# The low parts of 36 mixer weights, made during the feed-forward layer's way down and stored, instead of beside the recurrence

## The chip, the cores and the metric

The kernel runs on one core of one Trainium2 chip. The metric is the device time of one execution in microseconds (us). Six units are spoken of: PE (TensorE matmuls), PEld (TensorE's loading of weights, beside the matmuls), DVE (VectorE), ACT (ScalarE), POOL (GpSimd) and SP (SyncE, which issues almost every DMA here and does nothing else). Each takes its instructions in a fixed order and stops at the first one whose inputs aren't there.

## The reference

One layer of a diffusion transformer over 1152 columns (1024 latent tokens and 128 of context), width 1024, in fp32, for latents and context with the same weights:

```
x += 1/2 * gate1 * SwiGLU1(adaLN(RMSNorm(x)))        # first feed-forward half step
x += gate2 * W_out( sig(g_a)*Up_a(MLA(h)) + sig(g_r)*Up_r(HGRN2_bidir(h)) ),  h = adaLN(RMSNorm(x))
x += 1/2 * gate3 * SwiGLU2(adaLN(RMSNorm(x)))        # second feed-forward half step
...
def swiglu(h, w1, w3, w2):
    return (jax.nn.silu(h @ w1) * (h @ w3)) @ w2
...
qc, kvc, kr, hq, hf_f, hf_b, hi, hgate, ga, gr = jnp.split(h @ w_in, split_idx, axis=-1)
```

The change touches two places: the product with `w2` in the first half step (2816 hidden rows to 1024), called the way down, and the first 36 tiles of `w_in` (1024 x 128 each), which feed the HGRN2 recurrence and the gates `ga` and `gr`.

## The kernel before

Full fp32 accuracy is made out of three fp32r matmuls. A matrix A is split into a high part Ah (A rounded to fp32r, a cast on ACT) and a low part Al = A - Ah (a subtraction, mostly on POOL); the product is wh·xh + wh·xl + wl·xh (`mm3`, L455, L456, L457). Line 238 and line 239 in `hl` make the high and the low part of a weight tile; lines 1624 and 1625 those of a hidden tile (`hh`, `hl`).

The way down (`ffn_fast`, then `down_group` and `down_last`): 22 hidden tiles of 128 x 1152 are loaded from DRAM (`hr`, 576 KB), split (`hh`, `hl`), and multiplied with 22 rows of `w2` (`raw`, 512 KB, split into `wh`, `wl` for even and `wxh`, `wxl` for odd rows). They go in pairs: 9 groups of two tiles, called group 0 to 8 here, then `down_last` with the last four. A group has 24 ticks (8 row blocks m, 3 chunks of 384 columns); a tick is 6 matmuls into one bank (`dn`) and then one to three additions to `x` on DVE (L484), scaled from the bank. At every third tick a background generator (`self.bg`, `ada_sum`) takes one step: a load of 256 KB (`wada`) and a reduction on DVE (`junk`, L308). The bank has three buffers, hidden tiles two groups' worth, `wh` and `wl` three, `raw` two.

The recurrence (`hgrn`) runs the HGRN2 scans of eight heads level by level. DVE carries most of it (`KE`, `QP`, `T`, `A`), POOL takes part of it (`QP`, `Y`), and PE's small matmuls (`lv`, L860) wait for these. Beside it run 36 dense products, one per tile of `w_in` (`proj_f`, `proj_q`, `proj_v`, `proj_gate`, `proj_sg`); each loads its weight, casts `wh` on ACT and subtracts `wl` on POOL. For the very first tile the two halves of `wl` are made on DVE (`home="pieces"`).

The order of each engine's instructions is set once, when the program is built, by a scheduler that follows the order of the code, the priorities and the pools' buffers; at run time nothing passes anything on the same engine. All loads and stores spoken of here go through SP's queue.

Of the kernel before, what the change touches and what calls it, by code (L numbers as in the profile page):

```python
# [9 lines left out]
F32 = mybir.dt.float32  # L10
F32R = mybir.dt.float32r
# [8 lines left out]
P = 128  # L20
D = 1024
KT = D // P
# [8 lines left out]
ORDER = (2, 0, 1)  # L31
# [31 lines left out]
def rows(w, m):  # L63

    return w[m // 4][:, ts(m % 4, P)] if isinstance(w, list) else w[:, 0, ts(m, P)]
# [22 lines left out]
class Trunk:  # L88
# [1 line left out]
        self.tc, self.nc, self.a, self.o = tc, tc.nc, a, o  # L90

    def run(self):
        self.part, self.mode, self.chunks, self.bg = {}, "ffn1", ORDER, iter(())
        nc, tc, a = self.nc, self.tc, self.a
        with ExitStack() as st:
            self.cp = st.enter_context(tc.tile_pool(name="cp", bufs=1))
            self.wp = st.enter_context(tc.tile_pool(name="wp", bufs=1))
            self.tp = st.enter_context(tc.tile_pool(name="tp", bufs=25))
            self.dp = st.enter_context(tc.tile_pool(name="dp", bufs=1, space=DRAM))
            self.consts()  # L100
            self.xs = self.dp.tile([KT, P, T], F32, name="xs")
            self.modt = self.cp.tile([P, 9, KT, 2], F32, name="modt")
            self.gs = self.cp.tile([P, 3, KT, 2], F32, name="gs")
            with ExitStack() as s1:
                self.ffn_pools(s1)
                self.start()
                self.ffn_fast(0, 2, 1)
            self.mode = "mix"
            with tc.tile_pool(name="mp", bufs=1) as mp:
                self.mixer_consts(mp)  # L110
                self.mixer()
            with ExitStack() as s1:
                self.mode = "ffn2"
                self.ffn_pools(s1)
                self.merge()
                self.ffn_fast(1, 8, 3)
# [101 lines left out]
    def hl(self, raw, shape, eng=None, pin=lambda i: i, home=None):  # L218
        if home == "half":
            wh, wl = [[self.half(n, F32R)[:, : D // 2] for _ in range(2)] for n in ("wxh", "wxl")]  # L220
            for v in range(2):
                src = raw[:, 0, ts(v, D // 2)]
                self.nc.scalar.copy(wh[v], src)
                self.nc.gpsimd.tensor_sub(wl[v], src, wh[v])
            return wh, wl
        if home == "pieces":
            wh, wl = [self.wp.tile(shape, F32R, tag=t, bufs=3, name=t) for t in ("wh", "wl")]
            for v in range(2):
                k = slice(4 * v, 4 * v + 4)
                self.nc.scalar.copy(wh[:, k], raw[:, k])  # L230
                self.nc.vector.tensor_sub(wl[:, k], raw[:, k], wh[:, k])
            return wh, wl
        if home:
            wh, wl = [home(n)[:, :D].rearrange("p (o d) -> p o d", o=1) for n in ("wxh", "wxl")]
        else:
            wh = self.wp.tile(shape, F32R, tag="wh", bufs=3, name="wh")
            wl = self.wp.tile(shape, F32R, tag="wl", bufs=3, name="wl")
        pin(self.nc.scalar.copy(wh, raw))  # L238
        pin((eng or self.nc.gpsimd).tensor_sub(wl, raw, wh))  # L239
        return wh, wl  # L240

    def load_w(self, src, kt, m, pin=lambda i: i, home=None):
        raw = self.wp.tile([P, kt, m], F32, tag="raw", bufs=2, name="raw")
        self.nc.sync.dma_start(raw, src)
        return self.hl(raw, [P, kt, m], None, pin, home)
# [247 lines left out]
    def down_group(self, w2, fs, hs, gm, ws=None):  # L493
        ws = ws or [self.load_w(w2[f], 1, D) for f in fs]
        for m in range(KT):
            for c in self.chunks:
                self.down([(rows(wh, m), rows(wl, m)) for wh, wl in ws], hs, gm, c, m)
                self.ticks += 1
                if self.ticks % 3 == 0:
                    next(self.bg, None)  # L500

    def down_last(self, w2, fs, hs, gm, nxt):
        n = len(fs)
        self.new_rs()
        o = (0, 3, 1, 2)
        spare = "half" if nxt < 3 else partial(self.wide, dt=F32R)
        ws = [self.load_w(w2[fs[i]], 1, D, home=spare if i == 3 else None) for i in o]
        hs = [hs[i] for i in o]
        if nxt == 3:
            self.down_final(ws, hs, gm)  # L510
            return
        nc = self.nc
        if nxt == 2:
            self.alloc_b(1)
        else:
            self.alloc_h()
        tail = iter(())
        for c in self.chunks:
            cs = slice(*span(c))
            for m in range(KT):  # L520
                self.down([(rows(wh, m), rows(wl, m)) for wh, wl in ws], hs, gm, c, m)
                self.stat(c, m)
                nc.sync.dma_start(self.xs[m][:, cs], self.x[m][:, cs])
                if m:
                    next(tail, None)
            for _ in tail:
                pass
            tail = self.norm(c, nxt)
        self.tail = tail
# [103 lines left out]
    def proj_f(self, i, h, out):  # L633
        nc = self.nc
        fs = out["f"] = self.tt(F32, "fs")
        nc.vector.memset(fs[64:P, 0:1], 1.0)
        w = self.load_w(self.a["w_in"][i], KT, P, home="pieces" if i == 0 else None)
        for c in ORDER:
            s = self.sigm((yield from self.proj_g(w, c)))
            lo, hi = c * CW, (c + 1) * CW  # L640
            for r, o in ((slice(0, 64), 0), (slice(64, P), 1)):
                nc.scalar.activation(
                    fs[r, lo + o : hi + o], s[r], AF.Identity, scale=self.lb1[r, h : h + 1], bias=self.lb[r, h : h + 1]
                )
            yield

    def proj_q(self, i, out):
        q = out["q"] = self.tt(F32, "q")
        w = self.load_w(self.a["w_in"][i], KT, P)
        for c in ORDER:  # L650
            ps = yield from self.proj_g(w, c)
            self.nc.vector.tensor_mul(q[:, c * CW : (c + 1) * CW], ps, self.sigm(ps))  # L652
            yield

    def proj_v(self, i, out):
        nc = self.nc
        V = out["V"] = self.tt(F32, "V")
        w = self.load_w(self.a["w_in"][i], KT, P)
        for c in ORDER:
            ps = yield from self.proj_g(w, c)  # L660
            t = self.fp.tile([P, CW], F32, tag="t", bufs=3, name="t")
            nc.scalar.copy(t, ps)
            pt = self.pp.tile([P, CW], F32, tag="sm", bufs=3, name="vt")
            for j in range(3):
                nc.tensor.transpose(pt[:, ts(j, P)], t[:, ts(j, P)], self.ident)
            nc.scalar.copy(V[:, c * CW : (c + 1) * CW], pt)
            yield

    def proj_gate(self, i, p, oT):
        nc = self.nc  # L670
        w = self.load_w(self.a["w_in"][i], KT, P)
        sq = self.tt(F32, "osq")[:, :T]
        nc.scalar.activation(sq, oT[:, :T], AF.Square)
        for c in ORDER:
            ps = yield from self.proj_g(w, c)
            if c == ORDER[0]:
                self.lnexp()
                for b in ORDER:
                    self.rec_norm(b, oT, sq)
            s = self.sigm(ps)  # L680
            nc.vector.tensor_mul(s, ps, s)
            cs = slice(c * CW, (c + 1) * CW)
            nc.gpsimd.tensor_mul(s, oT[:, cs], s)
            nc.sync.dma_start(self.orec[p][:, cs], s)
            yield

    def proj_sg(self, j):
        w = self.load_w(self.a["w_in"][20 + j], KT, P)
        for c in ORDER:
            s = self.sigm((yield from self.proj_g(w, c)))  # L690
            self.nc.sync.dma_start(self.sg[j // KT, j % KT][:, c * CW : (c + 1) * CW], s)
            yield
# [876 lines left out]
    def ffn_fast(self, l, gm, nxt):  # L1569

        nc = self.nc
# [6 lines left out]
        for f in range(plain):  # L1578
# [7 lines left out]
            n = 0  # L1586
# [44 lines left out]
        for f in range(plain, NF):  # L1631
# [3 lines left out]
            for n in range(7):  # L1635
                if len(made) < 6:
                    w = next(ops, None)
                    if w:
                        made.append(w)
                w = made.pop(0)  # L1640
# [20 lines left out]
            self.put(*t)  # L1661
        self.x += [load_x(k) for k in range(2, KT)]
        if l == 0:
            self.bg = self.ada_sum((6, 7), lambda: self.bank("up", "cb", D // 2), partial(self.tt, F32), self.slim)
        for f in range(2, NF):
            pend.append(split_h(*load_h(f)))
            if f % 2 and f < NF - 1:
                fs, hs = zip(*pend[:2])
                self.down_group(w2, fs, hs, gm, ws or [load_w2(v) for v in fs])
                pend, ws = pend[2:], None  # L1670
        for _ in self.bg:
            pass
        fs, hs = zip(*pend)
        self.down_last(w2, fs, hs, gm, nxt)
# [122 lines left out]
```

## Time and the profile before

| what | value |
|---|---|
| median of 3 runs | 2986.64 us (2986.32 to 2988.35) |
| the profiled execution | 2991.17 us, span 2989.4 us |
| mean granted clock of TensorE | 0.986 of full |
| PE busy | 2882.2 us (96%) |
| DVE busy | 2034.1 us (68%) |
| ACT busy | 1242.1 us (42%) |
| POOL busy | 1084.1 us (36%) |
| groups 0 to 8 of the first way down | 558.0 to 785.9 us, 25.1 us a group |
| `down_last` | 785.9 to 839.4 us |
| the recurrence with its 36 products | 839.5 to about 1460 us |

Times inside the program are counted from the span's start. Where the table of a stretch gives an engine less busy time than the stretch is long, the rest is idle time; only PE's counts towards the end directly. In rows of the timeline the bracket at the end is how long the engine was idle before, and what ended that.

### The profile page before, as it was taken

Reading aid. Unit: us, or ns where it says so; the run is one execution under the profiler, and the core shown is the slowest. Engines: PE = TensorE matmul, PEld = TensorE weight load, DVE = VectorE, ACT = ScalarE, POOL = GpSimd, SP = SyncE. Lnnn points to the kernel's source line nnn. Section 1 sums busy time; section 2 is a strip of 40 time slices with the busy share of each in tenths; the row PEclk is TensorE's granted clock in tenths of the full one; section 3 lists DMA queues with packets and bytes.
Section 4 is the critical chain, followed back from the end, with each engine's and each line's share of the span. In section 5 each row is a group of like instructions: output and inputs, shape, how many; then the busy total and the mean of one; then the engine's idle time right before and its main releaser. Section 6 shows DMA issues by size and latency. Waiting matters only on the chain. (4 is left out here: it accounts for less than half of the span.)

```text
span 2989.4 us, 49363 instructions
## 1 busy us (share of the span) xinstructions
PE 2882.2 (96%) x18498; PEld 2737.8 (92%) x18498; DVE 2034.1 (68%) x4206; ACT 1242.1 (42%) x2375; POOL 1084.1 (36%) x979
## 2 busy tenths in 40 slices
PE   7999999999989999999998999989999999999998
PEld 5999999999989989898997887779999999999997
DVE  7787777677668787877456677766674665546665
ACT  5432332321274555555244777731362233232113
POOL 4132322454153333323234444532342322236434
PEclk8999999999999999999998999999999999999999
DMA  6643333743111111111210000242352322235211
GB/s 231 203 147 122 121 129 115 250 158 117 61 58 60 35 53 38 51 38 44 66 51 12 14 17 20 65 155 90 117 180 97 106 88 74 74 117 203 90 45 64
DMA packets 151471, 282.37 MB, mean 94 GB/s; under 512 B 19201, under 2 KB 83649, under 8 KB 151233
## 3 DMA queue, kind: packets, MB, share of 16 engines
q1 hardware_dynamic: 151088, 278.90, 28.2%
q8 instruction: 146, 2.39, 0.3%
q14 instruction: 93, 0.75, 0.1%
q10 hardware_dynamic: 144, 0.33, 0.0%
HBM read 215.64 MB, written 63.52 MB: 93 GB/s over the span
## 5 line engine op out<-in xcount | busy, mean ns | idle before, releaser
L1547 PE MATMUL b<-xo,wo 128*128 128x288 f32 x3552 | 484.7, 296 | 0.0
L1547 PEld LDWEIGHTS b<-xo,wo 128*128 128x128 f32 x3552 | 476.5, 188 | 0.0
L484 DVE SCALAR_TENSOR_TENSOR x<-dn,modt,x 128x256 f32<-128x256 f32 (+4 forms) x728 | 353.2, 505 | 167.9 <-PE dn L457 167.0
L239 POOL TENSOR_TENSOR wl<-raw,wh 128x1024 fp32r<-128x1024 f32 (+1 forms) x106 | 240.3, 2268 | 371.5 <-ACT wh L238 357.7
L455 PE MATMUL mm<-xh,wh 128*128 128x384 f32 (+1 forms) x1008 | 361.6, 359 | 5.7 <-DVE q L652 3.7
L1547 PE MATMUL b<-bh,wo 128*128 128x288 f32 x1776 | 365.2, 295 | 0.7 <-ACT et L1557 0.7
L457 PE MATMUL mm<-xh,wl 128*128 128x384 f32 (+1 forms) x1008 | 342.6, 340 | 1.7 <-POOL wl L239 1.5
L456 PE MATMUL mm<-xl,wh 128*128 128x384 f32 (+1 forms) x1008 | 343.0, 340 | 0.0
L1547 PEld LDWEIGHTS b<-bh,wo 128*128 128x128 f32 x1776 | 288.7, 188 | 1.0 <-ACT et L1557 0.9
L1547 PE MATMUL b<-bl,wo 128*128 128x288 f32 x888 | 261.6, 295 | 0.0
L1522 ACT CAST wo<-raw 128x512 fp32r<-128x512 f32 x185 | 114.8, 621 | 231.2 <-PE b L1547 114.5
L238 ACT CAST wh<-raw 128x1024 fp32r<-128x1024 f32 (+1 forms) x108 | 104.3, 967 | 250.6 <-PE dn L456 166.1
L455 PEld LDWEIGHTS mm<-xh,wh 128*128 128x128 f32 (+1 forms) x1008 | 190.9, 189 | 15.6 <-DVE q L652 4.5
L455 PE MATMUL dn<-hh,wh 128*128 128x384 f32 (+2 forms) x576 | 196.0, 340 | 2.6 <-DVE x L484 1.3
L1523 DVE TENSOR_TENSOR wo<-raw,wo 128x512 fp32r<-128x512 f32 x185 | 127.1, 688 | 102.2 <-ACT wo L1522 99.3
L457 PE MATMUL dn<-hh,wl 128*128 128x384 f32 (+2 forms) x576 | 194.2, 337 | 1.0 <-POOL wl L239 1.0
L456 PE MATMUL dn<-hl,wh 128*128 128x384 f32 (+2 forms) x576 | 194.1, 337 | 0.0
L457 PEld LDWEIGHTS mm<-xh,wl 128*128 128x128 f32 (+1 forms) x1008 | 190.4, 189 | 3.5 <-POOL wl L239 2.0
L456 PEld LDWEIGHTS mm<-xl,wh 128*128 128x128 f32 (+1 forms) x1008 | 190.9, 189 | 1.6 <-issue 0.4
L1625 POOL TENSOR_TENSOR hl<-hr,hh 128x1152 fp32r<-128x1152 f32 x44 | 118.0, 2692 | 196.9 <-ACT hh L1624 103.7
L1279 POOL TENSOR_TENSOR ehl<-e,ehl 128x512 fp32r<-128x512 f32 x93 | 123.3, 1330 | 142.9 <-ACT ehl L1277 77.3
L1518 POOL TENSOR_TENSOR ws<-raw 128x256 f32<-128x256 f32 x74 | 68.5, 945 | 292.9 <-DMA raw<-in_w 265.8
(385 smaller groups left out, 7284.9 us busy)
## 6 DMA issues: line engine op xcount, KB each, us to landing
raw<-in_w SPq DMA_DIRECT2D x148, 256.0 KB, 2.9
raw<-in_w SPq DMA_DIRECT2D x58, 512.0 KB, 3.6
wada<-in_w_aT SPq DMA_DIRECT2D x112, 256.0 KB, 2.9
hr<-hs SPq DMA_DIRECT2D x44, 576.0 KB, 5.1
hs<-et SPq DMA_DIRECT2D x148, 144.0 KB, 1.7
raw<-in_w_in SPq DMA_DIRECT2D x41, 512.0 KB, 3.5
hb<-hd SPq DMA_DIRECT2D x44, 288.0 KB, 3.4
x<-in_xT SPq DMA_DIRECT2D x16, 576.0 KB, 8.7
```

Of the source, the lines that this page charges most:

```text
L238: pin(self.nc.scalar.copy(wh, raw))
L239: pin((eng or self.nc.gpsimd).tensor_sub(wl, raw, wh))
L455: nc.tensor.matmul(ps, wh, xh, start=start and i == 0, stop=False)
L456: nc.tensor.matmul(ps, wh, xl, start=False, stop=False)
L457: nc.tensor.matmul(ps, wl, xh, start=False, stop=stop and i == n - 1)
L484: nc.vector.scalar_tensor_tensor(self.x[m][:, a:b], ps[:, a - lo : b - lo], self.modt[:, gm, m, s : s + 1], self.x[m][:, a:b], ALU.mult, A ...
L1279: eng.tensor_sub(el, e, eh)
L1518: nc.gpsimd.tensor_tensor(o[:, c], x[:, c], y[:, c], op)
L1522: nc.scalar.copy(wh, src[i])
L1523: nc.vector.tensor_sub(wl, src[i], wh)
L1547: nc.tensor.matmul(ps, w[:, k], x[:, k, :QW], start=first, stop=last, skip_group_check=home != i)
L1625: nc.gpsimd.tensor_sub(hl, raw, hh)
```

## The change

A second generator, `low_parts`, takes a step at every tick whose number leaves 1 when divided by 3. For each of the 36 weights it loads the raw tile once more (`wraw`, 512 KB), casts each half to a scratch (`whi`, 128 x 512, ACT), subtracts that in place (128 x 512, POOL), and stores the result (512 KB) to a new DRAM tile `wlo`. A weight's store is issued within the next weight's steps. In the recurrence `load_in` loads the raw tile as before and the low part from `wlo`, and casts `wh`; POOL's subtraction is gone, and so are DVE's two halves for the first tile.

```diff
             self.xs = self.dp.tile([KT, P, T], F32, name="xs")
+            self.wlo = self.dp.tile([36, P, D], F32, name="wlo")
...
-        if home == "pieces":
-            wh, wl = [self.wp.tile(shape, F32R, tag=t, bufs=3, name=t) for t in ("wh", "wl")]
-            for v in range(2):
-                k = slice(4 * v, 4 * v + 4)
-                self.nc.scalar.copy(wh[:, k], raw[:, k])
-                self.nc.vector.tensor_sub(wl[:, k], raw[:, k], wh[:, k])
-            return wh, wl
...
+    def load_in(self, i):
+
+        raw = self.wp.tile([P, KT, P], F32, tag="raw", bufs=2, name="raw")
+        wh, wl = [self.wp.tile([P, KT, P], F32R, tag=t, bufs=3, name=t) for t in ("wh", "wl")]
+        self.nc.sync.dma_start(raw, self.a["w_in"][i])
+        self.nc.sync.dma_start(wl.rearrange("p k m -> p (k m)").bitcast(F32), self.wlo[i])
+        self.nc.scalar.copy(wh, raw)
+        return wh, wl
+
+    def low_parts(self):
+
+        nc = self.nc
+        pin = self.tc.keep_in_program_order
+        src = lambda i: self.a["w_in"][i].rearrange("p k m -> p (k m)")
+        n = self.wlo.shape[0]
+
+        def load(i):
+            raw = self.tt(F32, "wraw")[:, :D]
+            nc.sync.dma_start(raw, src(i))
+            return raw
+
+        nxt, done = load(0), None
+        yield
+        for i in range(n):
+            raw = nxt
+            low = raw.bitcast(F32R)
+            if i + 1 < n:
+                nxt = load(i + 1)
+            for v in range(2):
+                c = ts(v, D // 2)
+                hi = self.half("whi", F32R)[:, : D // 2]
+                pin(nc.scalar.copy(hi, raw[:, c]))
+                pin(nc.gpsimd.tensor_sub(low[:, c], raw[:, c], hi))
+                if v == 0 and done:
+                    nc.sync.dma_start(*done)
+                yield
+            done = self.wlo[i], raw
+        nc.sync.dma_start(*done)
...
                 if self.ticks % 3 == 0:
                     next(self.bg, None)
+                elif self.ticks % 3 == 1:
+                    next(self.low, None)
...
-        w = self.load_w(self.a["w_in"][i], KT, P, home="pieces" if i == 0 else None)
+        w = self.load_in(i)
...
         if l == 0:
+            self.low = self.low_parts()
             self.bg = self.ada_sum((6, 7), lambda: self.bank("up", "cb", D // 2), partial(self.tt, F32), self.slim)
...
-        for _ in self.bg:
+        for _ in chain(self.bg, self.low):
             pass
```

(The four other calls of `load_w` in `proj_q`, `proj_v`, `proj_gate` and `proj_sg` become `load_in` in the same way.)

What that makes of the engines' orders, at three places. First ACT at the end of group 0, before. `hh_6271` and `hh_6277` are group 1's hidden tiles; `wxh_6524` is the high part of group 1's second weight, `wh_6754` that of group 2's first; `hh_6506` and `hh_6512` are group 2's hidden tiles, which take over buffers that group 0 reads to its end.

```order
L1624 CAST hh_6271<-hr_6269 128x1152
L1624 CAST hh_6277<-hr_6275 128x1152
L238 CAST wxh_6524<-raw_6522 128x1024
L238 CAST wh_6754<-raw_6752 128x1024
L1624 CAST hh_6506<-hr_6504 128x1152
L1624 CAST hh_6512<-hr_6510 128x1152
```

The same place on ACT after the change (`hh_6541` and `hh_6547` are group 2's hidden tiles, `wxh_6559` is group 1's second weight):

```order
L268 CAST whi_6393<-wraw_6330 128x512
L268 CAST whi_6424<-wraw_6330 128x512
L268 CAST whi_6455<-wraw_6391 128x512
L268 CAST whi_6486<-wraw_6391 128x512
L268 CAST whi_6517<-wraw_6453 128x512
L1660 CAST hh_6541<-hr_6539 128x1152
L1660 CAST hh_6547<-hr_6545 128x1152
L233 CAST wxh_6559<-raw_6557 128x1024
```

Group 1's second weight now stands behind group 2's hidden tiles, where it stood ahead of them; POOL's `hl` and `wxl` follow in the same order.

Second, SP's queue at the same place, after the change:

```order
L271 DMA wlo_92<-wraw_6391 128x1024
L323 DMA wada_6311<-in_w_aT 128x512
L1654 DMA hr_6539<-hs0_632 128x1152
L1654 DMA hr_6545<-hs0_632 128x1152
L278 DMA raw_6557<-in_w2 128x1024
```

The load of group 1's second weight follows a store that waits for POOL's sixth half step. In a middle group it stands the same way. Here is POOL between the second weight of group 2 (`wxl_6832`, one row ahead of the first) and that of group 3 (`wxl_7104`), after the change:

```order
L269 TENSOR_TENSOR wraw_6725<-wraw_6725,whi_6844 128x512
L269 TENSOR_TENSOR wraw_6787<-wraw_6787,whi_6875 128x512
L269 TENSOR_TENSOR wraw_6787<-wraw_6787,whi_6906 128x512
L1661 TENSOR_TENSOR hl_6814<-hr_6811,hh_6813 128x1152
L234 TENSOR_TENSOR wl_7098<-raw_7095,wh_7097 128x1024
L1661 TENSOR_TENSOR hl_6820<-hr_6817,hh_6819 128x1152
L269 TENSOR_TENSOR wraw_6873<-wraw_6873,whi_6937 128x512
L269 TENSOR_TENSOR wraw_6873<-wraw_6873,whi_6968 128x512
L269 TENSOR_TENSOR wraw_6935<-wraw_6935,whi_6999 128x512
L269 TENSOR_TENSOR wraw_6935<-wraw_6935,whi_7030 128x512
L269 TENSOR_TENSOR wraw_6997<-wraw_6997,whi_7061 128x512
L234 TENSOR_TENSOR wxl_7104<-raw_7101,wxh_7103 128x1024
```

and SP in that stretch:

```order
L271 DMA wlo_92<-wraw_6935 128x1024
L323 DMA wada_6311<-in_w_aT 128x512
L1654 DMA hr_7083<-hs0_632 128x1152
L1654 DMA hr_7089<-hs0_632 128x1152
L278 DMA raw_7101<-in_w2 128x1024
```

So `raw_7101`, from which `wxl_7104` is made, isn't issued before POOL has done the second half of `wraw_6935`.

Third, POOL in the recurrence, before, at one of the 36 weights (`wl_11683`; `QP` and `Y` are the scan's):

```order
L871 TENSOR_TENSOR QP_10595<-QP_10595,T64_11256 64x3x64
L819 TENSOR_TENSOR QP_11369<-Qb_11494,TQ_11531 128x384
L239 TENSOR_TENSOR wl_11683<-raw_11680,wh_11682 128x1024
L797 TENSOR_TENSOR Y_9034<-fs_11133,Y_9034 128x48 x3
L871 TENSOR_TENSOR QP_10595<-QP_10595,T8_11314 64x24x8
```

and after:

```order
L907 TENSOR_TENSOR QP_10918<-QP_10918,T64_11579 64x3x64
L855 TENSOR_TENSOR QP_11692<-Qb_11817,TQ_11854 128x384
L833 TENSOR_TENSOR Y_9359<-fs_11456,Y_9359 128x48 x3
L907 TENSOR_TENSOR QP_10918<-QP_10918,T8_11637 64x24x8
```

The subtraction is gone from POOL's row; on SP a load of the low part stands in its place.

More of the change, by code (lines that the diff above doesn't have):

```diff
@@ L92, in run @@
     def run(self):
-        self.part, self.mode, self.chunks, self.bg = {}, "ffn1", ORDER, iter(())
+        self.part, self.mode, self.chunks = {}, "ffn1", ORDER
+        self.bg = self.low = iter(())
         nc, tc, a = self.nc, self.tc, self.a
@@ L648, in proj_q @@
         q = out["q"] = self.tt(F32, "q")
-        w = self.load_w(self.a["w_in"][i], KT, P)
+        w = self.load_in(i)
         for c in ORDER:
@@ L657, in proj_v @@
         V = out["V"] = self.tt(F32, "V")
-        w = self.load_w(self.a["w_in"][i], KT, P)
+        w = self.load_in(i)
         for c in ORDER:
@@ L670, in proj_gate @@
         nc = self.nc
-        w = self.load_w(self.a["w_in"][i], KT, P)
+        w = self.load_in(i)
         sq = self.tt(F32, "osq")[:, :T]
@@ L687, in proj_sg @@
     def proj_sg(self, j):
-        w = self.load_w(self.a["w_in"][20 + j], KT, P)
+        w = self.load_in(20 + j)
         for c in ORDER:
```

## The prediction

> **What bounds the kernel now.** I read the page's table of engines first, then the table of stretches, and in the two stretches that the change touches the groups, the timeline and the waits.
>
> ```profile
> PE 2882.2 (96%) x18498; PEld 2737.8 (92%) x18498; DVE 2034.1 (68%) x4206; ACT 1242.1 (42%) x2375; POOL 1084.1 (36%) x979
> ```
>
> ```profile
> core 0: us, PE busy (x) PEld busy (x) DVE busy (x) ACT busy (x) POOL busy (x), PEclk, DMA share, GB/s
> 558.00:585.00 27.00, 26.02 (x147) 25.13 (x146) 19.82 (x48) 6.38 (x8) 10.07 (x4) 1.00 0.91 329
> 585.00:786.00 201.00, 201.00 (x1154) 201.00 (x1153) 157.38 (x377) 36.69 (x37) 86.41 (x35) 1.00 0.37 124
> 840.00:1460.00 620.00, 585.39 (x3628) 550.10 (x3628) 473.02 (x1038) 335.64 (x702) 207.42 (x241) 0.98 0.15 48
> ```
>
> PE is the bound everywhere. In groups 1 to 8 of the way down (585 to 786) it never rests: nothing can be won there, only lost. In the recurrence it rests for 620 - 585.4 = 34.6 us. The change takes work out of the second stretch and puts it into the first. So two questions: what of the 34.6 us is POOL's subtraction to blame for, and does the way down still feed PE?
>
> **The recurrence: what goes.** The 34 whole subtractions by POOL, PE's waits there, and one example on three engines in order of time:
>
> ```profile
> L239 POOL TENSOR_TENSOR wl<-raw,wh 128x1024 fp32r<-128x1024 f32 x34 | 81.5, 2399 | 151.4 <-ACT wh L238 151.4
> L872 DVE TENSOR_TENSOR T<-T 128x24 f32<-128x24 f32 x24 | 4.4, 183 | 1.1
> L814 DVE TENSOR_TENSOR T<-TK,TQ 128x48 f32<-128x48 f32 x24 | 22.5, 939 | 0.5
> PE lv L860 <- DVE QP L871: 17.2, 15, 2.3
> ```
>
> ```profile
> 1088.45 2.77 DVE L872 TENSOR_TENSOR T<-T 128x24 f32<-128x24 f32 x3
> 1088.84 2.37 POOL L239 TENSOR_TENSOR wl<-raw,wh 128x1024 fp32r<-128x1024 f32 x1 [0.48 <-ACT wh L238]
> 1098.02 1.62 PE L860 MATMUL lv<-QP,kr 128*128 128x128 f32 x6 [2.29 <-DVE QP L871]
> 1253.75 0.91 PE L860 MATMUL lv<-QP,kr 128*128 128x128 f32 x6 [2.32 <-DVE QP L871]
> 1409.05 0.91 PE L860 MATMUL lv<-QP,kr 128*128 128x128 f32 x6 [2.32 <-DVE QP L871]
> ```
>
> POOL's 81.5 us are off the path; what counts is DVE. Its three tiny `T` instructions take 2.77 us when POOL's `wl` starts among them, though one takes 0.18: they end when `wl` ends, 2.2 us late. DVE then never catches up before the scan's next step, and PE waits 2.29 us at 1098. The same pattern comes back twice, at 1253.8 and 1409.1. Without `wl` these 6.9 us go.
>
> ```profile
> 1098.10:1102.00 3.90, 3.90 (x17) 3.90 (x18) 3.72 (x11) 3.23 (x9) 2.36 (x4) 0.61 0.14 50
> 1255.00:1259.00 4.00, 4.00 (x18) 3.82 (x17) 3.77 (x12) 2.08 (x6) 2.76 (x5) 0.60 0.15 51
> 1409.00:1413.00 4.00, 3.01 (x18) 2.71 (x18) 3.82 (x11) 3.35 (x9) 2.30 (x4) 1.00 0.14 49
> ```
>
> After two of the three pauses the granted clock falls to 0.6 for about 3.4 us, which costs 3.4 x 0.5 = 1.7 us each, 3.4 together; after the third it doesn't. The Trainium skill (TensorE: Matmul & The Clock Gate, Part 1: The HAM clock gate) has the clock halved only after an idle window of about 3.4 us. By that, pauses of 2.3 us would cost no clock, and the gain would be 3.4 us smaller; the first two rows speak against it, so I go by the rows.
>
> At the start of the recurrence:
>
> ```profile
> 843.87 0.91 PE L427 MATMUL nps<-rs,ones 128*128 128x384 f32 x2 [1.61 <-DVE rs L373]
> 847.57 0.69 PE L457 MATMUL mm<-xh,wl 128*128 128x384 f32 x1 [1.51 <-POOL wl L239]
> 850.50 0.17 DVE L598 MEMSET onesb<- 128x128 f32 x1 [5.54 <-POOL xl L399]
> 862.16 0.66 PE L455 MATMUL mm<-xh,wh 128*128 128x384 f32 x1 [2.23 <-DVE q L652]
> ```
>
> PE waits 1.51 us for the second weight's `wl`, and 2.23 us for DVE, which had stood 5.54 us behind POOL's `xl` that queued behind `wl`. Both shrink: 3.7 us at most. Late next is the first low part: its load can only start when `down_last` lets go of a weight buffer, at about 839, and a 512 KB load takes 3.6 us (its row stands below), where DVE's halves held PE up for almost nothing. That overlaps the pause of 1.61 us that PE has there anyway, so I charge 2 us, and book the start at a net +1.7. Of the other DVE waits (17.2 - 6.9 = 10.3 us in 12) I take 4 us, since DVE is as much to blame there by its own load. The 36 extra loads are 18.9 MB on 48 GB/s over 620 us, 31 GB/s more: hidden. ACT's casts stay.
>
> Sum: 6.9 + 3.4 + 1.7 + 4 = 16, less 1 for waits of the scans on POOL's own `QP` that come next: **-15 us**. Bounds: -6 (only the three pauses go, and the clock falls elsewhere), -26 (all of the 17.2, 3.4 and 3.7, and a little more).
>
> **The way down: what comes.** Prices from the same stretch:
>
> ```profile
> L1625 POOL TENSOR_TENSOR hl<-hr,hh 128x1152 fp32r<-128x1152 f32 x20 | 53.6, 2689 | 94.9 <-ACT hh L1624 81.8 <-PE dn L456 11.9 <-DMA wada<-in_w_aT 1.1
> L239 POOL TENSOR_TENSOR wxl<-raw,wxh 128x1024 fp32r<-128x1024 f32 x8 | 19.4, 2425 | 19.4 <-ACT wxh L238 19.3
> L224 POOL TENSOR_TENSOR wxl<-raw,wxh 128x512 fp32r<-128x512 f32 x2 | 2.6, 1300 | 1.7 <-ACT wxh L223 1.7
> L1624 ACT CAST hh<-hr 128x1152 fp32r<-128x1152 f32 x20 | 23.0, 1155 | 105.4 <-PE dn L456 71.0 <-issue 22.1 <-DMA hr<-hs 12.3
> L238 ACT CAST wxh<-raw 128x1024 fp32r<-128x1024 f32 x8 | 8.4, 1053 | 48.9 <-DMA raw<-in_w 48.9
> L484 DVE SCALAR_TENSOR_TENSOR x<-dn,modt,x 128x384 f32<-128x384 f32 x143 | 88.1, 617 | 44.4 <-PE dn L457 44.2
> ```
>
> POOL: 72 halves x 1.30 = 94 us more over 225 us of nine groups; with its 86 + 10 it would be 84% busy. ACT: 72 x 0.62, hidden, since it is 18% busy. DVE: it adds from a bank, and its 617 ns hold also where POOL runs, so I price contention there at nothing. DMA: 36 loads and 36 stores of 0.524 MB are 37.7 MB over 225 us, 168 GB/s on top of 124. As averages all this fits. The order decides: each odd row of `w2` now passes SP behind a store that waits for POOL.
>
> *Group 1.* PE's first matmul of it, before, and the chain for its second weight, not in order of time:
>
> ```profile
> 584.88 0.33 PE L455 MATMUL dn<-hh,wh 128*128 128x384 f32 x1
> 574.42 1.83 SPq L244 DMA_DIRECT2D raw<-in_w  x2
> 579.09 1.05 ACT L238 CAST wxh<-raw 128x1024 fp32r<-128x1024 f32 x1 [6.36 <-DMA raw<-in_w]
> 580.21 2.41 POOL L239 TENSOR_TENSOR wxl<-raw,wxh 128x1024 fp32r<-128x1024 f32 x1 [3.60 <-ACT wxh L238]
> 584.42 2.21 ACT L1624 CAST hh<-hr 128x1152 fp32r<-128x1152 f32 x2 [2.86 <-PE dn L456]
> 571.30 5.30 POOL L1625 TENSOR_TENSOR hl<-hr,hh 128x1152 fp32r<-128x1152 f32 x2 [14.41 <-ACT hh L1624]
> ```
>
> `wxl` was ready at 582.6, 2.3 us before group 1 began at 584.9. Now POOL ends its `hl` pair at 576.6, then six halves, 576.6 + 6 x 1.3 = 584.4; only then does SP issue store, `wada`, two `hr` and `raw` (some 0.4 us each), so `hr` starts at 585.3.
>
> ```profile
> raw<-in_w SPq DMA_DIRECT2D x58, 512.0 KB, 3.6
> ...
> hr<-hs SPq DMA_DIRECT2D x44, 576.0 KB, 5.1
> 566.00:570.00 4.00, 4.00 (x25) 4.00 (x24) 2.72 (x6) 0.00 (x0) 0.00 (x0) 1.00 1.02 416
> ```
>
> `hr` lands at 590.4, `hh` at 591.6 and 592.7, `wxh` at 593.8; POOL's `hl`, `hl`, `wxl` end at 594.3, 597.0 and 599.4. PE has three triples without this weight and then needs it at 586.5: it stands still for 12.9 us, or 11 if `hr` lands after 3.6. I take 12, and 1.7 for the clock after such a pause: **+13.7** (9 to 16).
>
> *Groups 2 to 8.* Between one `wxl` and the next POOL must do three halves, `hl`, `wl`, `hl`, four halves: 3.9 + 2.7 + 2.4 + 2.7 + 5.2 = 16.9 us. Then SP's burst: store, `wada`, two `hr`, `raw` are 0.52 + 0.26 + 2 x 0.59 + 0.52 = 2.5 MB, which at the peak rate of 416 GB/s take 6.0 us, with 1.5 for issue and latency 7.5. Counted from its own issue, 1.7 us into the burst, `raw` then lands after 5.8 us. The nearest case before is a load behind two `hr` and a `wada`, with no store ahead of it:
>
> ```profile
> 601.24 0.33 SPq L244 DMA_DIRECT2D raw<-in_w  x1
> 606.07 1.05 ACT L238 CAST wxh<-raw 128x1024 fp32r<-128x1024 f32 x1 [7.33 <-DMA raw<-in_w]
> ```
>
> It took 4.8 us; the store and the `wraw` in flight are a megabyte more, so I stay with 5.8. Then come the cast, 1.05, and `wxl`, 2.4. The loop takes 16.9 + 7.5 + 1.05 + 2.4 = 27.9 us against PE's 25.1 a group. The pause at group 1 gives PE's feeders a start, so the first two groups lose about 0 and 1, the other five about 2.6: **+14**. Lower end: `raw` lands 3.6 us after its own issue (1.7 after the store), loop 25.7, +3. Upper end: 329 GB/s, the rate of group 0, +1.5 a group, and POOL delayed too: +25.
>
> The Trainium skill (SBUF — State Buffer, Summary: rules for kernel authors) reckons such transfers at about 358 GB/s. By that the burst takes 6.9 us, and five groups lose 0.9 us more each; the trace's 416 GB/s decides.
>
> In `down_last` I add nothing: POOL makes its weights right behind the last half, and two groups' pauses have given it time. Sum in the way down: 13.7 + 14 = **+27 us** (12 to 41).
>
> **The sum.** +27 - 15 = +12 us. On the profiled execution's 2991.2 that is 3003; the median of the runs is 4.5 us lower, so I forecast 2986.6 + 12 = **2998 us**, rounded down.
>
> **The rivals.**
> - *The loads come soon enough (faster).* If `raw` lands within 4 us of its issue, the loop is 25.7 to 26.1 us, groups 2 to 8 lose 3, the pause at group 1 costs 9 to 11, and the recurrence gives the upper part of its range, 23: 13 - 23 = -10, 2977 us. For it: the median landing is 3.6 us. Against it: that is in a stretch with 124 GB/s; in the burst three bigger transfers are ahead of it. It turns on the loop: at 26 us with 23 gained it is faster, at 28 it isn't.
> - *The two cancel (same).* Loop at 26 and group 1 as forecast, +16, against -15: 2987 us.
> - *The recurrence gives nothing (slower still).* DVE's freed time is eaten by waits that lie just behind (PE's first wait for the low part's load, `QP` on POOL): -2 with +27: 3012 us. Against it: the pauses at 1098, 1254 and 1409 have a visible cause.
>
> **How the numbers follow.** Chances: forecast 0.45, faster 0.2, same 0.2, recurrence without gain 0.15. A difference of 0.2% (6 us) is about what can be told from none here; so faster 0.2, same 0.2, slower 0.45 + 0.15 = 0.6. The range for 8 in 10 runs from the first rival's centre to the third's, half of each left out (0.1 and 0.08): 2978 to 3012 us. The forecast's own range is 2993 to 3006.
>
> **What would show it.** Right: PE idle for some 12 us about 2 us into group 1, ended by POOL's `wxl`; group starts about 28 us apart from group 4 on; SP waiting for POOL ahead of `hr` and `raw`; the pauses near 1098, 1254 and 1409 gone and DVE's `T` of 128 x 48 well under 939 ns. Wrong: groups 25.1 us apart (POOL or DMA faster than reckoned); DVE's additions above 617 ns (contention that I priced at nothing); or the long pauses still there, which would put them down to the scan's own chain and not to `wl`.

## The result, and the profile after

The changed kernel takes 3027.7 us (median of four runs, 3021.8 to 3030.7) against 2987.5 us before: 1.0132 times as long, 95% interval 1.0115 to 1.0150, or 40 us. 2998 us was forecast, 2978 to 3012 as the range: the sign was right and the size was not. The profiled execution took 3029.1 us, its span 3027.4.

The table of engines, then the table of stretches: groups 0 to 8 of the way down, one a row, then `down_last`, then the recurrence up to about the place that 1460 us was before.

```profile
PE 2895.5 (96%) x18498; PEld 2746.8 (91%) x18498; DVE 1995.0 (66%) x4204; ACT 1280.7 (42%) x2446; POOL 1085.6 (36%) x1016
```

```profile
558.20:587.50 29.30, 26.19 (x146) 24.82 (x145) 19.82 (x48) 7.25 (x11) 14.04 (x9) 1.00 0.83 291
587.50:627.70 40.20, 28.85 (x146) 28.02 (x146) 20.03 (x48) 11.83 (x17) 21.98 (x13) 0.83 0.79 283
627.70:655.40 27.70, 25.63 (x146) 25.34 (x145) 19.86 (x48) 5.74 (x9) 17.99 (x12) 1.00 0.71 249
655.40:685.70 30.30, 27.34 (x145) 26.42 (x145) 19.95 (x48) 10.22 (x16) 20.91 (x13) 0.94 0.71 257
685.70:715.90 30.20, 25.72 (x146) 25.09 (x145) 19.12 (x46) 9.58 (x16) 20.25 (x13) 1.00 0.75 261
715.90:750.75 34.85, 29.62 (x144) 28.76 (x145) 20.25 (x49) 10.89 (x16) 24.91 (x16) 0.85 0.65 231
750.75:782.90 32.15, 28.43 (x146) 27.81 (x146) 25.55 (x50) 10.88 (x14) 30.40 (x18) 0.89 0.78 271
782.90:808.20 25.30, 25.30 (x146) 25.30 (x145) 19.96 (x48) 9.50 (x14) 20.21 (x13) 1.00 0.84 311
808.20:836.10 27.90, 25.77 (x145) 24.94 (x144) 21.78 (x41) 6.46 (x8) 15.15 (x9) 1.00 0.53 184
836.10:889.60 53.50, 52.55 (x293) 51.36 (x292) 35.49 (x72) 30.09 (x59) 12.56 (x11) 1.00 0.27 95
889.60:1498.00 608.40, 581.62 (x3647) 548.98 (x3648) 427.03 (x1041) 337.49 (x705) 126.53 (x208) 0.99 0.24 79
```

The way down, from its first matmul to its last, took 839.4 - 558.0 = 281.4 us and now takes 889.6 - 558.2 = 331.4 us: **+50.0**. From there to the end of the span it was 2989.4 - 839.4 = 2150.0 us and is 3027.4 - 889.6 = 2137.8: **-12.2**. The change touches only the recurrence of that. Up to the same matmul, the last `lv` of the scans, it took 648.8 us and now takes 633.8 (before, then after):

```profile
839.40:1488.20 648.80, 614.15 (x3813) 578.19 (x3813) 484.87 (x1066) 344.12 (x721) 214.25 (x249) 0.98 0.15 48
889.60:1523.40 633.80, 607.02 (x3814) 573.97 (x3814) 436.73 (x1064) 344.49 (x721) 130.15 (x214) 0.99 0.24 79
```

So the gain is the 15 us of the forecast (2.8 us are lost again in stages that no edit touches), and the loss was nearly twice the forecast (+27).

In the ten rows of the way down PE is busy 295.4 us, where three rows of before (26.0 and 201.0 us, shown above, and 52.95 from 786 to 840 us) add up to 280.0. So 15.4 us of the 50 are matmuls that took longer, 13.8 of them in the four groups whose granted clock was below 1 (0.83, 0.94, 0.85, 0.89); the other 34.6 us are pauses. What PE waited for there, in the table of waits (us in total, times, longest):

```profile
PE dn L489 <- DVE x L518: 21.2, 12, 4.2
PE dn L489 <- ACT wxh L233: 8.0, 1, 8.0
PE dn L491 <- POOL wxl L234: 5.7, 3, 3.3
PE dn L491 <- POOL wl L234: 0.9, 1, 0.9
DVE junk L342 <- DMA wada<-in_w_aT: 21.3, 8, 5.2
```

The second and third rows are mostly group 1's second weight, as forecast. The first is new: PE waits for DVE's additions, which have to free one of its three banks. And DVE waits as long, 21.3 us, for the background's `wada`. One case in order of time, SP, then DVE and PE:

```profile
702.05 2.84 SPq L271 DMA_DIRECT2D wlo<-wraw  x2
704.95 1.26 SPq L1654 DMA_DIRECT2D hr<-hs  x2
706.31 0.42 SPq L278 DMA_DIRECT2D raw<-in_w  x1
706.83 0.38 SPq L323 DMA_DIRECT2D wada<-in_w_aT  x1
714.42 0.69 DVE L342 SCALAR_TENSOR_TENSOR junk<-wada,cb 128x512 bf16<-128x512 f32 x1 [5.01 <-DMA wada<-in_w_aT]
715.92 0.42 PE L489 MATMUL dn<-hh,wh 128*128 128x384 f32 x1 [4.00 <-DVE x L518]
```

SP stands at the stores until POOL is done, then issues everything at once; `wada` goes out at 706.8 and DVE can start 7.6 us later. All additions stand behind that reduction, and PE pauses 4.0 us.

In the recurrence DVE's `T` of 128 x 48 fell from 939 to 369 ns and the pause of 2.3 us to 1.0 us, while PE's wait for DVE at the start grew from 2.2 to 5.0 us:

```profile
L850 DVE TENSOR_TENSOR T<-TK,TQ 128x48 f32<-128x48 f32 x24 | 8.9, 369 | 0.5
1141.12 0.91 PE L896 MATMUL lv<-QP,kr 128*128 128x128 f32 x6 [1.00 <-DVE QP L907]
911.01 0.69 PE L489 MATMUL mm<-xh,wh 128*128 128x384 f32 x1 [5.04 <-DVE q L688]
```

### The profile page after: what moved, and what is told of

Same layout as the page of the kernel before. It is cut to its first block, busy times and chain, and to the rows that moved or that the text cites. A ratio compares the mean times of both kernels' runs of the same rounds, so it can differ in the third digit from the quotient of the medians.

```text
span 3027.4 us, 49694 instructions
## 1 busy us (share of the span) xinstructions
PE 2895.5 (96%) x18498; PEld 2746.8 (91%) x18498; DVE 1995.0 (66%) x4204; ACT 1280.7 (42%) x2446; POOL 1085.6 (36%) x1016
## 5 line engine op out<-in xcount | busy, mean ns | idle before, releaser
L234 POOL TENSOR_TENSOR wl<-raw,wh 128x1024 fp32r<-128x1024 f32 (+3 forms) x71 | 156.0, 2198 | 209.0 <-ACT wh L233 195.2
L342 DVE SCALAR_TENSOR_TENSOR junk<-wada,cb 128x512 bf16<-128x512 f32 x224 | 165.3, 738 | 26.8 <-DMA wada<-in_w_aT 25.9
L489 PE MATMUL dn<-hh,wxh 128*128 128x384 f32 (+2 forms) x480 | 164.3, 342 | 8.2 <-ACT wxh L233 8.0
L1554 POOL TENSOR_TENSOR ws<-raw 128x256 f32<-128x256 f32 x74 | 66.1, 913 | 295.4 <-DMA raw<-in_w 272.3
```

Of the source, the lines that this page charges most:

```text
L342: nc.vector.scalar_tensor_tensor(junk, ws[n % 2], 1.0, cs[s], ALU.mult, ALU.mult, accum_out=o)
L489: nc.tensor.matmul(ps, wh, xh, start=start and i == 0, stop=False)
L1554: nc.gpsimd.tensor_tensor(o[:, c], x[:, c], y[:, c], op)
```

## The experiments

"Way down" is the time from the stage's first to its last matmul in the kernel's trace, beside 281.4 us before; "rest" is from there to the span's end, beside 2150.0 before. "us" is the median over the runs, beside medians of before between 2987.5 and 2989.8. Profiles of one kernel and of another differ by some us in stages that no edit touches, so differences of the rest under 5 us are not read. "Scans" is the first part of the rest, up to the last `lv`, beside 648.8 before; down_only and quarters, whose recurrence makes all its low parts itself, have 649.5 and 647.0 there. What follows took 1500.6 to 1505.5 us in all these kernels, 1501.2 before.

| kernel | us | way down | rest | scans |
|---|---|---|---|---|
| the change | 3027.7 | 331.4 | 2137.8 | 633.8 |
| down_only | 3035.2 | 326.5 | 2153.0 | 649.5 |
| rec_only | 2982.5 | 286.1 | 2137.4 | 634.0 |
| wada4 | 3025.0 | 329.2 | 2136.7 | 633.3 |
| store_pool | 3023.7 | 326.2 | 2136.2 | 634.2 |
| late_start | 3019.5 | 324.2 | 2137.3 | 634.2 |
| no_store | 3014.0 | 314.2 | 2137.3 | 634.3 |
| wada4_modt_late | 3028.0 | 331.5 | 2135.5 | 634.2 |
| all4 | 2998.9 | 300.2 | 2137.7 | 634.4 |
| two_wada | 3004.3 | 309.1 | 2136.0 | 633.6 |
| modt_dve | 3008.3 | 311.2 | 2136.4 | 633.5 |
| no_late | 2994.9 | 300.0 | 2137.3 | 634.7 |
| half18 | 2984.8 | 281.6 | 2143.7 | 642.4 |
| pick18 | 2981.0 | 281.1 | 2141.2 | 635.7 |
| pick18_plain | 2987.3 | 289.3 | 2136.2 | 635.4 |
| pick3 | 2990.1 | 281.3 | 2144.9 | 644.4 |
| quarters | 2989.4 | 281.2 | 2149.6 | 647.0 |

**Each half of the change alone.** down_only puts `load_w` back in the recurrence; rec_only makes one low part and loads it every time.

```diff
 def load_in(self, i):                      # down_only
+    return self.load_w(self.a["w_in"][i], KT, P, home="pieces" if i == 0 else None)
...
-    self.nc.sync.dma_start(wl..., self.wlo[i])   # rec_only, and n = 1
+    self.nc.sync.dma_start(wl..., self.wlo[0])
```

> The low parts are made and stored in the way down as in the change, but the recurrence makes its own again, as before. Theory: the way down lost 50 us and the recurrence won 12, and the two are independent, so this kernel takes 2987 + 50 = 3037 us (3030 to 3045). Rival: part of the lost time is got back later in the program whatever the recurrence does; then it is well under 3030 us.

> One low part alone is made and stored; the recurrence loads that one 36 times in place of the 36 low parts (wrong values, same sizes and times). Theory: only the gain is left, 2987 - 12 = 2975 us (2971 to 2979), with the long pause of 2.3 us before the scan's step down to about 1 us. Rival, the forecast's own lower bound: 2981 us, if the gain seen in the changed kernel came from the delayed way down.

down_only takes 47 us more than before, and its way down is 45.1 us longer. rec_only takes 6 us less, not 12; but its rest is 12.6 us shorter and its scans 14.8, as in the change. The difference lies in the one low part that it still makes in groups 0 and 1: that alone lengthened its way down by 4.7 us. So the two halves add up to the change within 5 us. Neither rival holds; for rec_only that is read from its rest, since its time alone is near the 2981 us of the rival.

**One suspect at a time.** wada4 gives the background four buffers, loaded three steps ahead; store_pool issues the stores on GpSimd's queue; late_start starts the generator in group 1 with nine steps a group; no_store makes all low parts, but stores only the first.

```diff
-ws = [w2[:, :HD], w2[:, HD : 2 * HD]]                        # wada4
+ws = [t[:, o : o + HD] for t in w2 for o in (0, HD)]         # two wada tiles, four halves
...
-    nc.sync.dma_start(*done)                                 # store_pool
+    nc.gpsimd.dma_start(*done)
...
-elif self.ticks % 3 == 1:                                    # late_start
+if self.ticks > 24 and (self.ticks % 3 == 1 or self.ticks % 24 == 14):
...
-if v == 0 and done:                                          # no_store; done = self.wlo[0], raw
+if v == 0 and i == 1:
```

> The change, with four buffers in place of two for the background's wada loads, issued three steps ahead. Theory A: of the 50 us in the way down 21 are pauses of PE behind DVE's additions, which stand behind a reduction whose wada load is late in SP's burst; with the clock that they cost, about 28 us go, and this takes about 3000 us (2995 to 3006). Theory B: the burst's bandwidth and the store's wait set the pace anyway; the pauses move to the waits for the second weight, and it takes 3018 us or more.

> The change, with the 36 stores issued on GpSimd's own queue, so that SP never waits for POOL. Theory A (the wait in SP's queue is the cause): loads run ahead again, what is left is some 7 us at group 1 with its clock, 2987 - 12 + 9 = 2984 us (2978 to 2992). Theory B (the DMA traffic itself is the cause): still 20 us or more above before, 3007 us or more. Issuing on GpSimd itself may cost POOL time; that would show in POOL's halves.

> The change, with the generator's steps starting in group 1 instead of group 0 and nine steps a group, so that group 1's second weight stands ahead of group 2's hidden tiles again. Theory: the pause at group 1 (8.05 + 3.31 us and 3.7 us of slow clock, 15 together) goes and the denser steps cost a little: 3027 - 15 + 2 = 3014 us (3008 to 3020). Rival: POOL and the DMA traffic set the whole pace, and the loss turns up in later groups: 3022 us or more.

> The change with all 36 low parts made in the way down, but only the first stored, and that one loaded 36 times in the recurrence (wrong values, same sizes). SP no longer waits for POOL, and 18.4 MB of writes are gone; the loads stay. Theory (SP's waits for the stores are the largest part): left are group 1, some 8 us, the small additions on DVE, 2 to 10, and some late wada: 2988 - 12.6 + 20 = 2996 us (2988 to 3003). Rival (the 36 loads and POOL's work cost it): 3015 us or more.

I expected wada4 and store_pool to be close to a cure, and neither was. Both times are those of theory B; for store_pool its reason, the traffic itself, doesn't hold, as all4 shows below. In wada4 DVE's waits for `wada` are gone and others stand in their place (PE's waits in its way down):

```profile
PE dn L491 <- ACT wxh L233: 15.3, 4, 10.7
PE dn L493 <- POOL wxl L234: 11.3, 5, 3.9
PE dn L491 <- DVE modt L351: 7.6, 1, 7.6
PE dn L491 <- DVE x L520: 1.4, 3, 0.6
```

That is the loop of the forecast: with `wada` out of the way, the second weight ends 26.6 of some 36 us of pauses, 14.5 of them in group 1 and 12.1 in groups 3 to 6, and one pause of 7.6 us stands behind DVE's `adac`, which took 8.7 us there. Of store_pool's 45 us, group 1 is 12.6 (pauses of 7.4 us and the slow clock after them, where its theory had 7 with the clock). In the rest PE waited for DVE, and DVE mostly for `wada`. SP was still held, now by `wraw` and `hr` tiles that wait for a buffer of the common pool until a store has landed, and `wada` behind them. And once DVE ran one tiny addition for 12.89 us (DVE, then POOL, then PE):

```profile
748.64 12.89 DVE L347 TENSOR_TENSOR adac<-adac 128x16 f32<-128x16 f32 x1
747.38 2.67 POOL L1661 TENSOR_TENSOR hl<-hr,hh 128x1152 fp32r<-128x1152 f32 x1
750.01 2.35 POOL L234 TENSOR_TENSOR wl<-raw,wh 128x1024 fp32r<-128x1024 f32 x1
752.33 2.60 POOL L1661 TENSOR_TENSOR hl<-hr,hh 128x1152 fp32r<-128x1152 f32 x1
754.89 2.34 POOL L234 TENSOR_TENSOR wxl<-raw,wxh 128x1024 fp32r<-128x1024 f32 x1
757.20 2.47 POOL L269 TENSOR_TENSOR wraw<-wraw,whi 128x512 fp32r<-128x512 f32 x2
760.22 1.27 POOL L269 TENSOR_TENSOR wraw<-wraw,whi 128x512 fp32r<-128x512 f32 x1
761.94 0.66 PE L489 MATMUL dn<-hh,wh 128*128 128x384 f32 x1 [10.21 <-DVE modt L349]
```

late_start took 12.5 us out of group 1 (which took 27.7 us) and 2.5 out of group 0, and lost 7.9 again, 2.2 in groups 2 to 8 and 5.7 in `down_last`. no_store lost 32.8 us with one store left, in group 0, so its theory (2996 us) failed and its rival (3015) came close: 10.6 at group 1, 1.3 in group 0, and 16.7 in one late group, where `wada` stood in SP's queue behind a `raw` and two `wraw` that waited for POOL to free their buffers (DVE's wait and PE's):

```profile
726.62 0.69 DVE L341 SCALAR_TENSOR_TENSOR junk<-wada,cb 128x512 bf16<-128x512 f32 x1 [7.95 <-DMA wada<-in_w_aT]
PE dn L488 <- DVE x L517: 15.8, 6, 7.0
```

So each cause covers another: when one is taken out, what is late next ends the pause.

**All at once, and one put back each time.** all4 has late_start, wada4 and store_pool, and the background's small additions (`adac`, `modt`, `gs`) on POOL. wada4_modt_late is all4 with the stores on SP; two_wada, modt_dve and no_late put back one of the others.

```diff
-nc.vector.tensor_add(acc[:, i, 0], acc[:, i, 0], acc[:, i, 1])
-nc.vector.tensor_tensor(self.modt[:, ms[i]], acc[:, i, 0], b, ALU.add)
+eng.tensor_add(acc[:, i, 0], acc[:, i, 0], acc[:, i, 1])     # eng = nc.gpsimd
+eng.tensor_tensor(self.modt[:, ms[i]], acc[:, i, 0], b, ALU.add)
```

> The change with the late start, four wada buffers, and the background's last small additions (adac, modt, gs) on POOL in place of DVE; stores still in SP's queue. Theory: what is left is SP's wait for POOL ahead of each second weight, a loop of 28 to 29 us against 25.1, about 25 us; 2988 - 12.6 + 25 = 3000 us (2993 to 3008). Rival: that wait doesn't matter once the other three are gone: 2988 us or less.

> As the kernel with late start, four wada buffers and the small additions on POOL, and the stores on GpSimd's queue too, so that SP's order of loads doesn't hang on POOL. Theory: with all four causes gone the way down loses 5 us at most and the recurrence keeps its 12.6: 2980 us (2974 to 2988). Rival: POOL's load and the traffic themselves cost the way down 25 us or more: 3000 us or more.

> The best version so far (late start, small additions on POOL, stores on GpSimd's queue, 2999 us) with two wada buffers again in place of four. Theory: with SP's queue held at times by buffers, DVE stands behind late wada loads as in the change, some 10 us: 3009 us (3004 to 3016). Rival: with the stores gone from SP two buffers are enough: 2999 us, within 4.

> The best version so far with the background's small additions (adac, modt, gs) back on DVE. Theory: DVE is shut out while POOL runs on without a pause, for 8 to 13 us, and PE behind it: 3009 us (3004 to 3016), with a row of adac or modt of several us. Rival: the long rows are chance, 2999 us, within 4.

> The best version so far with the generator starting in group 0 again. Theory: group 1's second weight is again behind group 2's hidden tiles, 7 to 8 us with the clock, less 1 for the thinner steps later: 3006 us (3002 to 3012), with PE idle in two pieces of 5 and 2.5 us at group 1. Rival: the thinner steps give back all of it: 2999 us or less.

wada4_modt_late was to take 3000 us and took 3028.0. From group 1 to group 8 (585.2 to 822 us) PE waits there for the second weight alone, and the weights' loads took a median of 8.4 us to land:

```profile
PE dn L498 <- POOL wxl L234: 12.3, 7, 3.5
PE dn L496 <- ACT wxh L233: 10.5, 6, 4.1
raw<-in_w SPq DMA_DIRECT2D x17, 512.0 KB, 8.4
```

So the forecast's own chain, without any wait for `wada`, is enough to lose 36 us up to the end of group 8; the other 14 us of the 50 are lost in `down_last`.

all4 loses 18.8 us in the way down, between its two theories. Where it loses them tells more (groups 0 and 1, 2 to 5, 6 and 7, which begin at 710 and end at 773; another 5.3 us are lost in `down_last`):

```profile
557.20:608.00 50.80, 50.51 (x290) 50.13 (x289) 39.77 (x96) 17.43 (x24) 32.95 (x22) 1.00 0.96 348
608.00:710.00 102.00, 101.48 (x578) 100.84 (x576) 78.69 (x189) 39.69 (x56) 93.10 (x70) 1.00 0.85 311
710.00:773.00 63.00, 53.99 (x288) 53.41 (x288) 40.51 (x98) 21.31 (x28) 55.97 (x41) 0.92 0.77 273
```

For four groups POOL is busy 91% of the time and DMA moves 311 GB/s, and PE idles 0.5 us in all. Neither POOL's load nor the traffic costs PE anything as such there. Then `hr` loads come late, held in SP's queue by buffers whose stores are under way (24.6 us of waits). Against all4's 300.2 us of way down, stores back on SP cost 31 us, the additions back on DVE 11 (one `adac` of 9.2 us), two `wada` buffers 9, and the early start nothing, as its rival had it: no_late lost 11.5 us at group 1 and won as much back in the thinner steps later. The 31 us come from one edit, the stores' queue; each of these prices holds with the other three means in place.

**Fewer weights.** half18 is all4's means for every second weight; pick18 for 18 picked ones; pick18_plain the same 18 with the change's own means; pick3 three weights with the change's own means, one step a group. All four start in group 1.

```diff
+EARLY = (0, 2, 3, 1, 35, 34, 33, 5, 7, 32, 4, 10, 29, 9, 15, 26, 14, 23)   # pick18; pick3: (10, 15, 23)
 def load_in(self, i):
+    if i not in EARLY:
+        return self.load_w(self.a["w_in"][i], KT, P)
...
+    if self.ticks > 24 and (self.ticks % 6 == 1 or self.ticks % 24 == 16):
+        next(self.low, None)
```

> The best version so far with every second weight only: 18 low parts are made in the way down, at half the density, and 18 in the recurrence as before. Theory (the remaining 18 us of the way down come from wraw tiles that hold the T buffers until their stores land, so that hidden tiles load late): at half the density that goes, and half of the recurrence's gain stays: 2987 - 6 + 2 = 2983 us (2979 to 2988). Rival: the loss is proportional to the traffic: 2987 - 6 + 9 = 2990 us or more.

> As the kernel with 18 low parts made early (2985 us), but another 18: those whose subtraction ran just ahead of PE's pauses in the profile before (the first seven, and ten or so by their place in the scan's period, among them the three ahead of the pauses of 2.3 us). Theory (the gain hangs on where DVE is held up): nearly the whole 12.6 us with no loss in the way down, 2988 - 11 = 2977 us (2974 to 2981). Rival (the gain goes by the number of subtractions): 2985 us, as with every second weight.

> The same 18 picked weights, but with the change's own means: stores in SP's queue, two wada buffers, small additions on DVE. Theory (it is the density: with half of the work POOL is ahead of SP, and a store's wait holds nothing up): 2977 + 6 = 2983 us (2978 to 2990). Rival (each store's wait in SP's queue costs, whatever the density): half of the 50 us, 3000 us or more.

> The change for three weights alone: those whose subtractions ran 7 us ahead of the pauses of 2.3 us at 1096, 1251 and 1407. All else as in the change (stores in SP's queue, two wada buffers, small additions on DVE), one step a group from group 1 on. Theory: each pause falls from 2.3 to 1.0 us and the slow clock behind it goes, 3 x 1.3 + 3.4 = 7 us, and the way down loses 1 or 2: 2982 us (2979 to 2985). Rival: the gain is spread over all 36, and three give 1 us: 2987 us.

At half the density the way down loses nothing (281.6 and 281.1 us), so the loss isn't proportional to the traffic. With the change's own means the same 18 weights cost 8 us (pick18_plain), so its rival, 3000 us or more, fails: density is most of it. How the 8 us divide between the stores' queue, the `wada` buffers and the small additions was not separated. half18 also shows that each of the three long pauses hangs on its own weight. The weight ahead of the pause that ended at 1098 us before was made early in it, those ahead of 1254 and 1409 were not:

```profile
1094.20 0.91 PE L905 MATMUL lv<-QP,kr 128*128 128x128 f32 x6 [0.98 <-DVE QP L916]
1240.14 2.38 POOL L234 TENSOR_TENSOR wl<-raw,wh 128x1024 fp32r<-128x1024 f32 x1 [0.48 <-ACT wh L233]
1249.34 0.91 PE L905 MATMUL lv<-QP,kr 128*128 128x128 f32 x6 [2.30 <-DVE QP L916]
```

pick18 is the fastest kernel here: 2981.0 us, 0.9972 of before, interval 0.9962 to 0.9982 (half18: 0.9992, 0.9984 to 1.0001). By time that is midway between its theory, 2977, and its rival, 2985. The scans decide for the theory: half18 gains 6.4 us there and pick18 13.1, of the 15.0 that all 36 weights give. Its table over the whole way down has PE busy for all but 1.4 us, at full clock:

```profile
555.40:836.50 281.10, 279.75 (x1589) 278.04 (x1588) 211.87 (x492) 92.38 (x138) 165.59 (x110) 1.00 0.59 207
```

pick3's three pauses fell to 0.98 us, as its theory says, with no loss in the way down, but the time didn't fall measurably (1.0003, 0.9994 to 1.0011); its profile alone has a rest 5 us shorter and gains 4.4 us in the scans, where its theory had 7. What the three weights are worth stays open.

**Smaller pieces in place.** quarters is the kernel before with each subtraction in the recurrence cut into four.

```diff
+for v in range(4):
+    k = slice(2 * v, 2 * v + 2)
+    self.nc.gpsimd.tensor_sub(wl[:, k], raw[:, k], wh[:, k])
```

> The kernel before, with POOL's subtraction of the 35 low parts in the recurrence cut into four of a quarter each, back to back. Theory A (DVE gets in only when POOL pauses): no change, 2988 us, within 4. Theory B (DVE gets in after each POOL instruction): it waits 0.6 us in place of up to 2.4 and wins half of the 12.6 us that the recurrence gained without these: 2982 us.

No change in time, as theory A has it, but not by its mechanism. DVE did get in between the pieces (POOL ran four from 1086.66 to 1089.46):

```profile
1087.45 0.65 DVE L882 TENSOR_TENSOR Gall<-T 128x3 f32<-128x3 f32 x1
1088.02 1.83 DVE L913 SCALAR_TENSOR_TENSOR S<-S,Gall,dS 64x64 f32<-64x64 f32 x3
```

But each of its short instructions then waited for a piece of its own, so the chain of them was hardly shorter (the pause was 1.94 us in place of 2.3), and POOL's pieces took 2.8 us in all, against 2.4.

## Why the prediction was wrong, point by point

*The recurrence: -15 forecast, -15.0 measured* (up to the last `lv`). The cause was right: without `wl` DVE's `T` is short again and the pauses shrink. That the sum fits is luck, for its terms were off both ways. In the two rows shown with the result PE's idle time fell by 7.8 us (34.6 to 26.8), where the waits were to give 6.9 + 1.7 + 4 - 1 = 11.6; its busy time fell by 7.1 us (614.2 to 607.0), where 3.4 had been charged for the clock. The three pauses gave 3 x 1.3 rather than 6.9 us, since a wait of 1.0 us for the same `QP` lay behind; all of PE's waits for DVE's `QP` gave 5.2 us, where 6.9 + 4 were charged. The first low part's load held PE 1.29 us (2 were charged). The wait for DVE's `q` at the start didn't shrink but grew to 5.04 us. And waits for ACT's `t`, which no term had, fell by 3.2 us (before, then two rows of after):

```profile
PE vt L665 <- ACT t L662: 4.3, 4, 2.0
PE lv L896 <- DVE QP L907: 12.0, 12, 1.7
PE vt L701 <- ACT t L698: 1.1, 4, 0.6
```

Why the one grew and the other fell stays open.

*Group 1: +13.7 forecast, +15.0 measured* (40.2 - 25.1). The order read off ACT, POOL and SP gave the place, the weight that PE waits for and the pause (11.4 us, 12 forecast; 8.05 of them for the cast `wxh`, 3.31 for `wxl`). That the pause fits so well is partly luck: the weight was ready 2.5 us later than forecast (601.9 us, not 599.4), and group 1 began 2.6 us later too, since group 0 lost 2.4 us to a late `wada`. The clock after it cost 3.7, not 1.7.

*Groups 2 to 8: +14 forecast, +32.7 measured* ((836.1 - 627.7) - 7 x 25.1). This is the step that failed: the loop of 27.9 us a group, ended by the second weight. It has three parts:

1. Left out: what else stands in SP's queue behind the waiting store. The prediction counted `wada` as bytes of the burst and never asked who waits for it. DVE does, the additions stand behind it, and PE has three banks: 18 us of the pauses from group 2 on, and 21 in all with group 0, where I had expected nothing. The second weight, which I had made the end of each loop, ended only 2.4 us of pauses there. But this wait alone is not what the change lost: without it the way down still takes 329.2 us (wada4), and the forecast loop appears, at 29 to 31 us a group in groups 3 to 5 where 27.9 had been reckoned. In wada4_modt_late, with nine steps a group in place of eight, it is 28.2 to 33.6 us in groups 2 to 7. So the loop was too short in itself, by the next two parts, and in the change the late `wada` covers it.
2. Mis-sized: landings under load. `raw` took 6.9 us, not 5.8, and `wada` 4.9 (3.1 between 585 and 786 us before). In the case shown above `raw` landed 9.1 us after the store was issued (704.6 to 713.7 us), where 7.5 had been reckoned; the 1.5 us for issue and latency in that term stood on no row:

```profile
raw<-in_w SPq DMA_DIRECT2D x19, 512.0 KB, 6.9
wada<-in_w_aT SPq DMA_DIRECT2D x28, 256.0 KB, 4.9
```

3. Mis-sized: the clock. In the way down I priced it once, 1.7 us, for group 1; it cost 13.8 us in four groups, some 10 of them in groups 3, 5 and 6, for which I had nothing. The Trainium skill (TensorE: Matmul & The Clock Gate, Part 1: The HAM clock gate) puts the fall after an idle window of about 3.4 us; the groups at 587.5 and 715.9, with pauses of up to 8.05 and 4.18 us, agree, but the ones at 655.4 and 750.8 fell to 0.94 and 0.89 with none longer than 1.87 and 2.75 us, and the one at 558.2 kept 1.00 with a pause of 2.56 us.

*"DVE: I price contention there at nothing"* held for the additions that read a bank (616 ns, as before), and failed for two instructions that the term didn't look at: the background's `adac` and `modt`. In the change they took 2.2 and 3.7 us; in other kernels up to 12.9.

The range missed because its upper end for the loop (+25) varied the landing alone and kept the same chain. The rivals missed alike: the slowest of them had 3012 us, from a recurrence that gives nothing, and none had a longer loop or another thing in SP's queue as the one that is late.

## What to carry to other kernels

Work that is free on average is paid for in the queue it is issued through. When a load or store that waits is put into an in-order queue, list everything behind it, and for each item who waits for it and how many buffers that one has; the item that ends up late need not be the one that the change is about. Taking out one cause of a delay and finding the time unchanged doesn't clear it: another, as long, may stand behind it. Background work that cost 50 us here cost 8 at half the density, and nothing once its stores, buffers and small additions were moved as well; half of it, chosen by which instructions ran just ahead of the pauses, brought 13.1 of the 15.0 us that the recurrence had to give (8.8 us in the medians).

## What the runs showed of the hardware that was not expected

A DVE addition of 128 x 16 with both inputs in SBUF took 12.89 us (748.64 to 761.53). It began inside one of POOL's subtractions, POOL ran six more, and it ended 0.04 us after the last; between the last two POOL had only issued a store (759.62 to 760.19), and the addition did not end there. On POOL it takes 0.2 us. The Trainium skill (SBUF — State Buffer, Summary: rules for kernel authors) has the second one to issue blocked until the first finishes, for a DVE instruction with two inputs in SBUF and a GpSimd instruction that reads SBUF; that fits quarters, where DVE got in after each piece of 0.7 us, and is less than what the 12.89 us show, which outlast the subtraction under way and six others. Why it got in at once there and not here was not settled.
